# Router rows, embedding weights and bias rows in other buffers, a fifth raw buffer, and the router's products of four token tiles interleaved

## Chip, cores and metric

The kernel runs on one core of a Trainium2 chip. The metric is device microseconds of one execution; the time of a kernel is the median of its runs. TensorE (PE) does the matrix products, VectorE (DVE), ScalarE (ACT) and GpSimd (POOL) the work on their results; SyncE (SP) issues most of the loads. The launch covers two layers of a transformer trunk, 512 tokens of width 1024, everything in fp32.

## The reference, cut to what matters

```python
for i in range(DEPTH):                       # 2 layers
    a = rmsnorm(h, g_mix[i])
    proj = a @ w_in[i]                       # q, k, v of three head groups
    oa = axial_gqa(qa, ka, va)               # group a
    ob = neighbourhood_attn(qb, kb, vb, na_bias[i])   # group b: relative bias
    oc = dilated_mixture(qc, kc, vc)         # group c
    h = h + concat(rmsnorm(oa), rmsnorm(ob), rmsnorm(oc)) @ w_out[i]
    h = h + expert_choice_ffn(rmsnorm(h, g_ffn[i]), w_router[i], w_gate[i], w_up[i], w_down[i])
    gate = sigmoid(rmsnorm(h, g_ple[i]) @ w_ple_gate[i])
    h = h + gate * (p[i] @ w_ple_proj[i])    # per-layer embedding, 256 -> 1024

def expert_choice_ffn(h, w_router, w_gate, w_up, w_down):
    aff = softmax(h @ w_router)              # 512 tokens x 16 experts
    gates, idx = top_k(aff.T, 64)            # each expert chooses 64 tokens
    xg = h[idx]
    hid = silu(xg @ w_gate) * (xg @ w_up)
    return segment_sum((hid @ w_down) * gates, idx)
```

The queries and keys of every head are normalized by their root mean square first. Group b adds a bias that depends on the distance of query and key and is cut by a mask.

## The kernel before

A layer is one long program, written in the order in which TensorE is to do it.

The input projection goes in seven blocks (cq, ck, cv, a, bq, bk, bv). A block (`Project`, L379) runs over 8 parts of the depth and 4 token tiles, with three matmuls for each, into banks 0 to 3. The three are there because a weight part is split into a rounded high part (a cast on ScalarE, L350) and the rest (a subtraction on POOL, L351); the pieces are the tiles `ch`, four of them. When a token tile of a q or k block is complete, `fin_qk` (L548) takes it out of its bank: a square into a "square" tile (2 buffers, L552), from which VectorE forms sums, and a copy into a "raw" tile (4 buffers, L550 and L553), which the transposes of the heads read later. The next block needs the same bank. The softmax work of the groups c, a and b is woven in behind the matmuls as side items.

Group b's bias is made on POOL (`prep_b`, L856): for each pair of heads an add of bias rows and a mask piece. The bias rows of the six heads are one tile of 1590 columns ("heads"), loaded by POOL at the layer's start (L874); the three mask pieces lie in two "square" buffers and one "w" buffer and are loaded by SP (L879). The calls stand in `bias_b`, at step 5 of block bv (`BIAS_AT`).

The output projection follows in six pieces (po[0] to po[5]). Behind its last piece stands the router: `router_T` (L934) transposes a half of one token tile of h and copies it into one of two half slots `hs`; `router_mm` (L951) multiplies the eight parts of one token tile by the router's weights, 32 columns of weights at a time. The four token tiles take the four column groups of the array, `tile_position=(0, 32 * t)`, and write to four strips of bank 0. `tail` (L960) calls both as token tiles become ready, and L984 to L986 do the rest. The logits are copied out of the bank (L1010), become probabilities, and VectorE and TensorE rank the tokens of each expert (L1037, L1050).

The experts come in eight pairs, each with 12 weight chunks of 2 MB (gate, up, down, four each). TensorE uses a chunk for 8 fp32 matmuls of 512 columns, 16 instructions in the trace. The class `Slots` plans the loads: one list of wanted chunks (`plan`, L267), a buffer ("slot") for each, and a load on SP's queue (L144) as soon as a slot is free for the first of the list. There are 9 slots of their own and two that are lent once the attention's memory is free ("early", "lent"). `keep(n)` holds back n half slots from the list, `take` hands out a half slot, `give` returns it. The load of the embedding's weights (1 MB, key "pp") stands in the same list ahead of pair 5, since `ple_proj` (L1139) uses them in that pair, on half slots too: one for the input and its transposes, two for the result.

## Time and profile before

| | |
|---|---|
| median of 3 runs | 1619.06 us (1618.86 to 1619.22) |
| the profiled execution's own time | 1618.79 us |
| its span in the profile | 1617.0 us (the other 1.8 us lie around it) |
| mean granted clock of TensorE | 0.986 |
| busy: TensorE, its weight loads | 1528.5 us (95%), 877.6 us (54%) |
| busy: VectorE, ScalarE, POOL | 713.1 us (44%), 489.1 us (30%), 278.9 us (17%) |
| moved by DMA | 469.81 MB, mean 291 GB/s |
| chain that ended last | TensorE 22%, DMA 12%, VectorE 3% |

The page's table of slices divides the span into 40 pieces of 40.4 us, which show the stages of both layers. Below that the trace has rows of single instructions, grouped where the same line follows itself: the time at which a group starts, how long it lasts, and in brackets the idle time of the engine ahead of it with what ended that. A fp32 matmul with 128 columns shows as two instructions ("passes"), so the router's 32 matmuls of a layer are 64 in the trace. A share over the whole span is a mean over these stages, so each stage is read by itself.

### The profile page before, as it was taken

Reading aid. Unit: us, or ns where it says so; the run is one execution under the profiler, and the core shown is the slowest. Engines: PE = TensorE matmul, PEld = TensorE weight load, DVE = VectorE, ACT = ScalarE, POOL = GpSimd, SP = SyncE. Lnnn points to the kernel's source line nnn. Section 1 sums busy time; section 2 is a strip of 40 time slices with the busy share of each in tenths; the row PEclk is TensorE's granted clock in tenths of the full one; section 3 lists DMA queues with packets and bytes.
Section 4 is the critical chain, followed back from the end, with each engine's and each line's share of the span. In section 5 each row is a group of like instructions: output and inputs, shape, how many; then the busy total and the mean of one; then the engine's idle time right before and its main releaser. Section 6 shows DMA issues by size and latency. Waiting matters only on the chain. (4 is left out here: it accounts for less than half of the span.)

```text
span 1617.0 us, 20229 instructions
## 1 busy us (share of the span) xinstructions
PE 1528.5 (95%) x7819; PEld 877.6 (54%) x7819; DVE 713.1 (44%) x1885; ACT 489.1 (30%) x1151; POOL 278.9 (17%) x282
## 2 busy tenths in 40 slices
PE   7999999999999987998999999998999998889988
PEld 7866777633443333333898677775344342333346
DVE  4757856442442322221476678563432342222143
ACT  6466545201101002011664655442101000021044
POOL 4413344000000000000544133530000000000013
PEclk9999999899999999999999999999999999899999
DMA  8003154899999999999401122468999999999961
GB/s 308 20 21 114 34 197 171 327 395 428 426 427 427 428 426 428 427 428 422 159 33 40 40 94 65 166 260 338 418 427 427 428 427 428 425 427 427 427 261 52
DMA packets 46176, 469.81 MB, mean 291 GB/s; under 512 B 7104, under 2 KB 9088, under 8 KB 19456
## 3 DMA queue, kind: packets, MB, share of 16 engines
q1 hardware_dynamic: 41296, 454.15, 68.6%
q0 software_dynamic: 3744, 13.16, 2.2%
q10 hardware_dynamic: 1040, 1.21, 0.3%
q8 instruction: 61, 1.00, 0.2%
q14 instruction: 35, 0.29, 0.1%
HBM read 461.04 MB, written 6.29 MB: 289 GB/s over the span
## 5 line engine op out<-in xcount | busy, mean ns | idle before, releaser
L235 PE MATMUL bank<-slots,xt 128*64 128x512 f32 x2048 | 460.6, 602 | 21.4 <-DMA slots<-in_w_up_dram 13.6
L235 PE MATMUL bank<-ch,slots 128*128 128x384 f32 (+1 forms) x2064 | 472.2, 372 | 8.0 <-ACT raw L553 5.3
L235 PEld LDWEIGHTS bank<-ch,slots 128*128 128x128 f32 x2064 | 360.2, 189 | 83.4 <-issue 38.9
L235 PEld LDWEIGHTS bank<-slots,xt 128*64 128x64 f32 x2048 | 143.9, 138 | 308.5 <-issue 272.3
L351 POOL TENSOR_TENSOR ch<-slots,ch 128x384 fp32r<-128x384 f32 (+1 forms) x172 | 199.8, 1169 | 328.9 <-ACT ch L350 304.8
L235 PE MATMUL bank<-slots,hid 128*64 128x512 f32 x1024 | 227.4, 598 | 13.1 <-DMA slots<-in_w_down_dram 10.0
L235 PEld LDWEIGHTS bank<-slots,hid 128*64 128x64 f32 x1024 | 72.6, 137 | 156.8 <-issue 139.6
L1195 DVE SCALAR_TENSOR_TENSOR hid<-bank,st,hid 128x512 f32<-128x512 f32 x32 | 23.8, 750 | 283.5 <-PE bank L235 274.6
L1086 POOL DMA_INDIRECT xg<-rows,ids x14 | 13.8, 986 | 724.1 <-DVE ids L1059 638.7
L350 ACT CAST ch<-slots 128x384 fp32r<-128x384 f32 (+1 forms) x172 | 95.5, 563 | 87.5 <-PE bank L235 64.7
L1130 DVE TENSOR_TENSOR h<-h,bank 128x512 f32<-128x512 f32 x128 | 79.9, 682 | 84.8 <-PE bank L235 84.8
L1229 DVE SCALAR_TENSOR_TENSOR xg<-bank,st,hid 128x512 fp32r<-128x512 f32 x32 | 22.6, 746 | 212.3 <-ACT hid L1228 212.3
L1191 ACT ACTIVATE hid<-bank,st 128x512 f32<-128x512 f32 x32 | 22.0, 687 | 264.5 <-PE bank L235 264.5
L235 PE MATMUL bank<-slots 64*128 64x512 f32 (+2 forms) x304 | 93.9, 558 | 0.9 <-DVE sa L679 0.9
L1037 DVE SCALAR_TENSOR_TENSOR less<-bank,tgv,order 128x512 bf16<-128x512 f32 x128 | 87.6, 747 | 15.8 <-PE bank L238 15.8
L1098 ACT ACTIVATE xt<-bank,gcols 128x128 f32<-128x128 f32 x56 | 20.4, 367 | 204.5 <-PE bank L238 202.8
L681 ACT ACTIVATE p<-p,sa 128x512 f32<-128x512 f32 (+1 forms) x96 | 58.8, 613 | 72.8 <-DVE sa L679 72.6
L1228 ACT ACTIVATE hid<-bank,st 128x512 fp32r<-128x512 f32 x32 | 20.3, 684 | 177.2 <-issue 144.1
L356 DVE SCALAR_TENSOR_TENSOR slots<-bank,gcols,slots 128x128 fp32r<-128x128 f32 (+1 forms) x160 | 53.4, 373 | 44.6 <-ACT slots L355 44.1
L238 PE MATMUL bank<-ident,p 128*128 128x128 f32 x416 | 63.0, 274 | 3.6 <-ACT slots L608 3.0
L355 ACT ACTIVATE slots<-bank,gcols 128x128 fp32r<-128x128 f32 (+1 forms) x160 | 53.9, 400 | 29.7 <-PE bank L235 18.2
L238 PEld LDWEIGHTS bank<-ident,p 128*128 128x128 f32 x416 | 50.5, 140 | 15.7 <-ACT slots L608 3.7
(139 smaller groups left out, 1442.8 us busy)
## 6 DMA issues: line engine op xcount, KB each, us to landing
slots<-in_w_gate_dram SPq DMA_DIRECT2D x64, 2048.0 KB, 28.4
slots<-in_w_up_dram SPq DMA_DIRECT2D x64, 2048.0 KB, 31.2
slots<-in_w_down_dram SPq DMA_DIRECT2D x64, 2048.0 KB, 32.4
slots<-in_w_in_dram SPq DMA_DIRECT2D x24, 768.0 KB, 5.8
slots<-in_w_ple_gate_dram SPq DMA_DIRECT2D x8, 1024.0 KB, 33.1
slots<-in_w_out_dram SPq DMA_DIRECT2D x6, 1024.0 KB, 6.0
slots<-in_w_in_dram SPq DMA_DIRECT2D x4, 1024.0 KB, 11.5
rows<-h POOLq DMA_DIRECT2D x8, 512.0 KB, 4.6
```

The source lines that it names most:

```text
L235: return placed(T.matmul(*a, **k))
L238: return placed(T.transpose(*a))
L350: S.copy(hi.bitcast(F32R), src)
L351: G.tensor_tensor(lo.bitcast(F32R), src, hi, ALU.subtract)
L355: S.activation(hi.bitcast(F32R), b, AF.Copy, scale=g)
L356: V.scalar_tensor_tensor(lo.bitcast(F32R), b, g, hi, ALU.mult, ALU.subtract)
L681: S.activation(pv, pv, AF.Exp, bias=nm, scale=-1.0, accum_out=ls)
L1037: V.scalar_tensor_tensor(ph.pool.tile([128, 512], BF16, tag="less", name="less", bufs=2), bk[6 + j], aff[:, t, e:e + 1], order[:, 128 * (3 ...
L1130: V.tensor_tensor(h[:, t, 512 * c:512 * c + 512], h[:, t, 512 * c:512 * c + 512], b, ALU.add)
L1191: S.activation(hid[:, c], bk[c], AF.Silu, scale=rslot[:, pr:pr + 1])
L1195: V.scalar_tensor_tensor(hid[:, c], bk[2 + c], rslot[:, pr:pr + 1], hid[:, c], ALU.mult, ALU.mult)
L1229: V.scalar_tensor_tensor(y[1][:, c], bk[4 + c], gatec[:, pr:pr + 1], y[0][:, c].bitcast(F32), ALU.mult, ALU.subtract)
```

## The change

Four things move, in both layers.

1. The embedding's weights leave the list of chunks. They get a tile of their own ("pp", 2048 columns) in the experts' phase, loaded on SP's queue at the start of that phase (L1007 of the new kernel).
2. `fin_qk` has five raw buffers. The bias rows no longer have a tile: they use two "square" and four "raw" buffers, and two of the mask pieces the values tile "va" of group a. So their loads stand in block bv, behind the last readers of these buffers, and the second pair's bias work moves from step 5 to step 7 of bv. The shifted values `vsh` get three tiles of their own.
3. The router's transposed rows get a phase and two tiles of their own ("rows0", "rows1"), in place of two half slots; no half slots are held back for them.
4. `router_mm` does all four token tiles in one go, the part outside, the token tile inside, so that neighbouring matmuls go to different column groups. It is called once, when all transposes are done.

```diff
--- before.py
+++ after.py
@@ -289,8 +289,6 @@
                      w_out[l, 128 * s:128 * s + 128, :].rearrange("(k q) f -> q k f", q=64)) for s in range(2)])
         mat(("out",), w_out[l], (1,))
         for e in range(0, NE, 2):
-            if e == 2 * EMBED:
-                chunks(("pp",), w_ple_proj[l])
             for name, w in (("g", w_gate), ("u", w_up), ("d", w_down)):
                 for i in range(4):
                     slots.want((l, name, e, i), [(lambda t: t, w[l, e // 2, i])])
@@ -547,7 +545,7 @@
 
         def fin_qk(t):
 
-            raw[t] = pa.tile(384, "raw", 4)
+            raw[t] = pa.tile(384, "raw", 5)
             sq = pa.tile(384, "square", 2)
             S.activation(sq, bk[MAIN[t]][:, 0:384], AF.Square)
             S.copy(raw[t], bk[MAIN[t]][:, 0:384])
@@ -856,29 +854,30 @@
         def prep_b(hd):
             bm = bmt[hd % 2]
             for i, off in ((0, 248), (1, 256), (2, 264)):
-                src = bias["raw"][:, hd, :]
+                src = bias["raw"][hd]
                 sv = bass.AP(tensor=src.tensor, offset=src.offset + off, ap=[list(src.ap[0]), [-1, 32], [-31, 8]])
                 G.tensor_tensor(bm[:, 256 * i:256 * i + 256].rearrange("q (j r) -> q j r", r=8), sv,
                                 bias["mask"][i].rearrange("q (j r) -> q j r", r=8), ALU.add)
 
         bmt = [pa.tile(768, f"bias{i}") for i in range(2)]
-        bias["raw"] = pa.tile(1590, "heads").rearrange("q (a n) -> q a n", a=6)
+        vsh = [pa.tile(384, f"shift{i}") for i in range(3)]
 
         def bias_b():
 
             side.drain()
             slots.give(ptx.pop())
             bias["vbt"] = slots.take()
-            bias["mask"] = [pa.tile(384, n, b)[:, 0:256] for n, b in (("square", 2), ("square", 2), ("w", 1))]
+            bias["raw"] = [pa.tile(384, n, b)[:, 0:265] for n, b in [("square", 2)] * 2 + [("raw", 5)] * 4]
+            va2 = pa.tile(512, "va")
+            bias["mask"] = [va2[:, 0:256], va2[:, 256:512], pa.tile(384, "w")[:, 0:256]]
             for hd in range(6):
-                G.dma_start(out=bias["raw"][:, hd, :],
+                G.dma_start(out=bias["raw"][hd],
                             in_=bass.AP(tensor=na_bias.tensor,
                                         offset=na_bias.offset + l * (NABIAS + 2 * BPAD) + BPAD + 465 * hd - 16,
                                         ap=[[1, 16], [31, 8], [1, 265]]))
             for i in range(3):
                 nc.sync.dma_start(out=bias["mask"][i], in_=cst_maskb[:, 256 * i:256 * i + 256])
             prep_b(0)
-            prep_b(1)
 
         def fin_vb(t):
             if "v" not in bias:
@@ -888,9 +887,8 @@
 
         layer.fin["bv"] = fin_vb
         now, late = post_qk(0, 6, 2, "b", 0, bqk[1])
-        pj["bv"].run(merge(then, now, {BIAS_AT: [bias_b]}))
+        pj["bv"].run(merge(then, now, {BIAS_AT: [bias_b], 7: [lambda: prep_b(1)]}))
         vb = bias["v"]
-        vsh = [pa.tile(384, "raw", 4) for i in range(3)]
         for i in range(3):
             S.dma_start(out=vsh[i][0:64, :], in_=vb[64:128, i, :])
             S.dma_start(out=vsh[i][64:128, :], in_=vb[0:64, i + 1, :])
@@ -934,8 +932,6 @@
         sh = ph.tile(8, "sh").rearrange("q (f t) -> q f t", f=2)
 
         def router_T(t, f):
-            if not hs:
-                hs.extend(slots.take() for _ in range(2))
             b = bk[1 + (t + f) % 3]
             for j in range(4):
                 k = 4 * f + j
@@ -948,10 +944,13 @@
             S.activation(unused(512), h[:, t, 512 * f:512 * f + 512], AF.Square,
                          accum_out=sh[:, f, t:t + 1])
 
-        def router_mm(t):
+        def router_mm():
+
             for k in range(8):
-                mm(bk[0][32 * t:32 * t + 32, 0:128], wr[:, k, :], four(hs[k // 4])[:, k % 4, 128 * t:128 * t + 128],
-                   start=k == 0, stop=k == 7, tile_position=(0, 32 * t))
+                for t in range(4):
+                    mm(bk[0][32 * t:32 * t + 32, 0:128], wr[:, k, :],
+                       four(hs[k // 4])[:, k % 4, 128 * t:128 * t + 128],
+                       start=k == 0, stop=k == 7, tile_position=(0, 32 * t))
 
         def free_b(n):
             if n > 11:
@@ -961,8 +960,6 @@
             G.dma_start(out=rows[128 * t:128 * t + 128, :], in_=h[:, t, :])
             if t > 0:
                 router_T(t - 1, 1)
-            if t > 1:
-                router_mm(t - 2)
 
         group["b"] = Attention("b", six(*bqk), [ptx[0][:, 512 * i:512 * i + 512] for i in range(4)])
         side.start(group["b"].items(free_b, group["a"].scale), PACE[2], LEAD[2])
@@ -978,20 +975,23 @@
         pa.close()
         phY = Phase("early", "right")
         slots.lend(phY.pool, NEARLY)
-        slots.keep(2)
+        slots.keep(0)
+        phR = Phase("router")
+        hs.extend(phR.tile(2048, f"rows{f}") for f in range(2))
         po[4].run({2: [group["b"].scale]}, po[5])
         po[5].run({i: [lambda t=t: router_T(t, 0) for t in ((0, 1), (2,), (3,))[i]] for i in range(3)})
         router_T(3, 1)
-        router_mm(2)
-        router_mm(3)
+        router_mm()
         slots.give(*mts[2:])
         if stop == "attn":
+            phR.close()
             break
 
 
         V.tensor_scalar(sh[:, 0], sh[:, 0], 1.0 / D, EPS, ALU.mult, ALU.add)
         V.scalar_tensor_tensor(ms4, sh[:, 1], 1.0 / D, sh[:, 0], ALU.mult, ALU.add)
         rsqrt(rtok, ms4, ta4, tb4)
+        phR.close()
         ph.close()
         phT = Phase("pt")
         pos = phT.tile(64, "pos").rearrange("q (t e) -> q t e", t=4)
@@ -1000,10 +1000,11 @@
         phX = Phase("lent")
         slots.lend(phX.pool, NLENT)
         ph = Phase("moe")
-        slots.give(*hs)
         slots.keep(0)
         G.iota(tgv[:, :, 0], pattern=[[128, 4]], base=0, channel_multiplier=1,
                allow_small_or_imprecise_dtypes=True)
+        wpp = ph.tile(2048, "pp")
+        nc.sync.dma_start(out=wpp, in_=w_ple_proj[l, 0])
         iot = ph.tile(64, "iot")
         G.iota(iot, pattern=[[1, 64]], base=0, channel_multiplier=0, allow_small_or_imprecise_dtypes=True)
         lg = ph.tile(512, "oh")[:, 0:128]
@@ -1137,7 +1138,7 @@
                 S.copy(pT[:, k, :], bk[6 + k])
 
         def ple_proj():
-            wp = slots.get((l, "pp", 0)).rearrange("q (k f) -> q k f", k=2)
+            wp = wpp.rearrange("q (k f) -> q k f", k=2)
             n = 0
             for t in range(4):
                 for f in range(2):
@@ -1147,7 +1148,6 @@
                         mm(b, pT[:, k, 128 * t:128 * t + 128], wp[:, k, 512 * f:512 * f + 512],
                            start=k == 0, stop=k == 1)
                     S.copy(ppv(t, f), b)
-            slots.done((l, "pp", 0))
 
         def halves(t):
             return t.rearrange("q (c n) -> q c n", c=2)
```

TensorE's order at the router of layer 0, before (bank_64 is bank 0 with the logits, bank_71 the output projection's last bank, `h` the transposes' source, slots_2569 the router's rows):

```order
L238 MATMUL bank_67<-ident,h 128x128 x4
L235 MATMUL bank_64<-slots_2569,wr 32x128 x8
L235 MATMUL bank_71<-ch,slots_908 128x512 x3
L238 MATMUL bank_65<-ident,h 128x128 x4
L235 MATMUL bank_64<-slots_2569,wr 32x128 x12
L238 MATMUL bank_66<-ident,h 128x128 x4
L235 MATMUL bank_64<-slots_2569,wr 32x128 x12
L238 MATMUL bank_69<-ident,oh 128x128
```

and now:

```order
L238 MATMUL bank_67<-ident,h 128x128 x4
L235 MATMUL bank_71<-ch,slots_908 128x512 x3
L235 MATMUL bank_64<-rows_2512,wr 32x128
L238 MATMUL bank_65<-ident,h 128x128 x4
L235 MATMUL bank_64<-rows_2512,wr 32x128 x4
L238 MATMUL bank_66<-ident,h 128x128 x4
L235 MATMUL bank_64<-rows_2512,wr 32x128 x11
L235 MATMUL bank_64<-rows_2513,wr 32x128 x16
L238 MATMUL bank_69<-ident,oh 128x128
```

The eight matmuls of the first two token tiles that stood ahead of bank_71's last three products are gone from there; 27 of the 32 now stand behind the last transposes (bank_66), where 12 stood.

ScalarE's order at the end of block bk (L552 and L553 are the square and the copy of `fin_qk`, bank_67 its last token tile, L672 exponentials of another group), before:

```order
L745 ACTIVATE squares<-bank_70 128x256
L350 CAST ch<-slots_110 128x384
L552 ACTIVATE square<-bank_67 128x384
L350 CAST ch<-slots_110 128x384
L319 ACTIVATE sa<-sa 128x24
L320 ACTIVATE sa<-sa 128x24
L672 ACTIVATE p,sa<-bank_68,sa 128x512
L672 ACTIVATE p,sa<-bank_69,sa 128x512
L553 COPY raw<-bank_67 128x384
L708 COPY slots_754<-bank_70 128x4x128
```

and now, where the same lines are two lower:

```order
L743 ACTIVATE squares<-bank_70 128x256
L348 CAST ch<-slots_110 128x384
L550 ACTIVATE square<-bank_67 128x384
L551 COPY raw<-bank_67 128x384
L348 CAST ch<-slots_110 128x384
L317 ACTIVATE sa<-sa 128x24
L318 ACTIVATE sa<-sa 128x24
L670 ACTIVATE p,sa<-bank_68,sa 128x512
L348 CAST ch<-slots_571 128x384
L670 ACTIVATE p,sa<-bank_69,sa 128x512
L706 COPY slots_754<-bank_70 128x4x128
```

The copy into raw has moved up to its square; before, it stood behind a cast, two small activations and two exponentials. The same move is found at the ends of ck and bq. POOL's order in block bv is, before (L351 are splits of weight parts, L861 the bias adds):

```order
L351 TENSOR_TENSOR ch<-slots_110,ch 128x384 x2
L351 TENSOR_TENSOR ch<-slots_571,ch 128x384 x4
L351 TENSOR_TENSOR ch<-slots_110,ch 128x384 x4
L861 TENSOR_TENSOR bias_1714<-heads,square 128x256
L861 TENSOR_TENSOR bias_1715<-heads,square 128x256
L351 TENSOR_TENSOR ch<-slots_571,ch 128x384 x2
```

and now:

```order
L349 TENSOR_TENSOR ch<-slots_571,ch 128x384 x4
L349 TENSOR_TENSOR ch<-slots_110,ch 128x384 x2
L874 DMA square<-in_na_bias_dram 128x1x265
L349 TENSOR_TENSOR ch<-slots_110,ch 128x384 x2
L874 DMA square<-in_na_bias_dram 128x1x265
L859 TENSOR_TENSOR bias_1714<-square,w 128x256
L859 TENSOR_TENSOR bias_1715<-square,w 128x256
L349 TENSOR_TENSOR ch<-slots_571,ch 128x384
L874 DMA raw<-in_na_bias_dram 128x1x265
L349 TENSOR_TENSOR ch<-slots_571,ch 128x384 x3
L874 DMA raw<-in_na_bias_dram 128x1x265
```

The bias rows' loads and the first pair's adds (with the mask piece "w", before at about 151 us) now stand between the splits of bv.

SP's order from the hand-over to the experts, before (the slots' numbers only tell buffers apart):

```order
L144 DMA slots_2503<-in_w_up_dram 128x4096
L144 DMA slots_2567<-in_w_up_dram 128x4096
L144 DMA slots_2702<-in_w_down_dram 128x4096
L144 DMA slots_2720<-in_w_down_dram 128x4096
L144 DMA slots_2725<-in_w_down_dram 128x4096
L144 DMA slots_2797<-in_w_down_dram 128x4096
L144 DMA slots_2821<-in_w_gate_dram 128x4096
L144 DMA slots_2841<-in_w_gate_dram 128x4096
```

and now:

```order
L144 DMA slots_2507<-in_w_up_dram 128x4096
L144 DMA slots_2572<-in_w_up_dram 128x4096
L144 DMA slots_2578<-in_w_down_dram 128x4096
L144 DMA slots_2712<-in_w_down_dram 128x4096
L144 DMA slots_2731<-in_w_down_dram 128x4096
L1007 DMA pp<-in_w_ple_proj_dram 128x2048
L144 DMA slots_2808<-in_w_down_dram 128x4096
L144 DMA slots_2832<-in_w_gate_dram 128x4096
```

The embedding's weights stand behind three "down" chunks of the first pair; before, they stood between a "down" chunk and the first "gate" chunk of pair 5.

## Rows read from the trace of the kernel before

**Rows 1.** Page, mean DMA rate in the span's 40 slices of 40.4 us

```profile
GB/s 308 20 21 114 34 197 171 327 395 428 426 427 427 428 426 428 427 428 422 159 33 40 40 94 65 166 260 338 418 427 427 428 427 428 425 427 427 427 261 52
```

**Rows 2.** Windows: length, busy of PE, PEld, DVE, ACT, POOL; clock, DMA share, GB/s

```profile
292.00:293.00 1.00, 1.00 (x7) 0.77 (x6) 1.00 (x2) 0.24 (x1) 0.03 (x1) 1.00 0.00 0
305.00:310.00 5.00, 3.10 (x13) 2.70 (x14) 3.70 (x11) 0.70 (x1) 0.00 (x0) 0.50 1.02 433
317.00:318.00 1.00, 1.00 (x8) 0.41 (x6) 0.00 (x0) 0.00 (x0) 0.00 (x0) 1.00 0.00 0
320.00:325.00 5.00, 5.00 (x29) 2.36 (x29) 0.00 (x0) 0.63 (x2) 0.00 (x0) 1.00 0.89 338
400.00:440.00 40.00, 40.00 (x198) 16.70 (x196) 17.33 (x49) 3.68 (x8) 0.98 (x1) 1.00 1.01 427
720.00:760.00 40.00, 36.15 (x167) 11.99 (x168) 3.87 (x12) 2.86 (x5) 0.00 (x0) 1.00 1.01 426
1105.00:1110.00 5.00, 3.04 (x16) 2.80 (x15) 5.00 (x17) 0.00 (x0) 0.00 (x0) 0.69 1.02 435
```

**Rows 3.** Timeline of SP's queue: start, us, load, count

```profile
296.95 22.32 SPq L144 DMA_DIRECT2D slots<-in_w_down_dram  x4
...
503.31 10.20 SPq L144 DMA_DIRECT2D slots<-in_w_up_dram  x3
...
537.67 0.33 SPq L144 DMA_DIRECT2D slots<-in_w_ple_proj_dram  x1
```

**Rows 4.** Timeline of TensorE near the end of layer 0's experts

```profile
757.15 3.65 PE L235 MATMUL bank<-slots,hid 128*64 128x512 f32 x16 [1.17 <-DMA slots<-in_w_down_dram]
```

**Rows 5.** Page, DMA issues: count, size of one, median us to landing

```profile
slots<-in_w_up_dram SPq DMA_DIRECT2D x64, 2048.0 KB, 31.2
```

**Rows 6.** TensorE's waits (total, times, longest), and timelines at block bk's end

```profile
PE bank L235 <- ACT raw L553: 5.3, 6, 1.4
...
192.01 0.47 ACT L553 COPY raw<-bank 128x384 f32<-128x384 f32 x1
...
192.53 0.80 PE L235 MATMUL bank<-ch,slots 128*128 128x384 f32 x3 [1.38 <-ACT raw L553]
```

**Rows 7.** Timelines of TensorE and VectorE at layer 0's router

```profile
294.09 1.93 PE L235 MATMUL bank<-slots,wr 128*32 128x128 f32 x16
295.95 0.97 PE L235 MATMUL bank<-ch,slots 128*128 128x512 f32 x3
...
299.62 0.66 PE L238 MATMUL bank<-ident,h 128*128 128x128 f32 x4
300.21 2.40 PE L235 MATMUL bank<-slots,wr 128*32 128x128 f32 x24
...
296.96 0.75 DVE L911 SCALAR_TENSOR_TENSOR h<-bank,sa,h 128x512 f32<-128x512 f32 x1 [2.09 <-PE bank L235]
```

**Rows 8.** Groups by line and shape: count, busy, mean ns, idle before

```profile
L235 PE MATMUL bank<-tgv,pick 128*128 128x18 f32 x128 | 15.8, 257 | 3.5 <-DVE pick L1050 3.5
L235 PE MATMUL bank<-slots,wr 128*32 128x128 f32 x128 | 13.5, 274 | 0.0
L235 PE MATMUL bank<-slots,raw 128*64 128x128 f32 x96 | 8.4, 280 | 0.0
L235 PEld LDWEIGHTS bank<-slots,wr 128*32 128x32 f32 x128 | 11.9, 110 | 1.0 <-issue 1.0
```

**Rows 9.** Timelines of POOL and TensorE in bv; landing of the bias rows (L874)

```profile
194.00 1.01 POOL L351 TENSOR_TENSOR ch<-slots,ch 128x384 fp32r<-128x384 f32 x1 [3.62 <-ACT ch L350]
...
208.03 1.33 PE L235 MATMUL bank<-ch,slots 128*128 128x384 f32 x6
...
DMA to landing us min/median/max: 4.6/6.1/7.7
```

**Rows 10.** Timelines of TensorE at the rank behind the router, layers 0 and 1

```profile
308.87 6.33 PE L235 MATMUL bank<-pick,h 128*128 128x128 f32 x28 [1.73 <-DVE pick L1050]
...
1107.21 4.88 PE L235 MATMUL bank<-pick,h 128*128 128x128 f32 x28 [1.96 <-DVE pick L1050]
```

## Prediction, made before the change was run

> **What bounds the kernel now.** I read the slices of the page first, to see which of the two long resources is short where. Each of the two layers has a stretch of about 400 us at 422 to 428 GB/s, and before it four slices of attention, 160 us, with 20 to 114 GB/s [rows 1]. Then I cut windows at the borders of these stretches [rows 2]: between 400 and 440 us the DMA engines are busy the whole time (share 1.01, 427 GB/s), and at 720 to 760 they still are (426 GB/s), while TensorE has 3.85 us of gaps in 40. Ahead of that, 292 to 293 and 317 to 318 show DMA share 0 while TensorE is full, and 320 to 325 only 338 GB/s. So each layer has three regimes: attention, where TensorE's order counts and DMA hardly; the hand-over to the experts (about 290 to 340 us in layer 0), where loads wait for buffers; and the expert stream, where only bytes count. The loads on SP's queue say why [rows 3]: from 296.95 to 319 us four loads go out, as slots come free; in the stream three issues 10.20 us apart from first to last (the last itself takes 0.33) are 4.93 us per 2 MB chunk, which is 2.10 MB at 427 GB/s, and TensorE ends the stretch waiting for chunks that have just landed [rows 4].
>
> This gives the prices: a byte in the stream costs its time at 427 GB/s, a byte in the hand-over is free while the engines have gaps, and a microsecond that TensorE saves between attention and the first expert moves the start of the stream and counts in full.
>
> **The change, part by part.** The sum is made against the profiled execution, 1618.79 us, which is 0.27 below the median of 1619.06. What a measurement of this kernel can tell from no change is about 0.2%, 3.2 us.
>
> *Embedding weights.* One load of 1 MB per layer leaves the stream, where it stood at 537.67 us [rows 3], and goes out ahead of the experts, behind the loads of the hand-over on SP. Out of the stream it saves 1.05 MB at 427 GB/s, 2.46 us. In its new place it takes 2.46 us of engines that stood idle around 317 and ran at 338 GB/s after 320: 20 us at 338 instead of 427 GB/s leave room for 1.8 MB. Nothing is due there: SP's next load waits for TensorE to release a slot anyway. Two layers: **-4.9**. Bounds: 0 (the stream waits for something else) and -4.9.
>
> *One weight slot more ahead of the router, one fewer behind pair 5.* The router's transposed rows no longer sit in half slots, so one "down" chunk can go out some 18 us sooner and fill the gap at 292 us. But the chunks that fit before TensorE frees the first one are as many as before (before, the router's slot came back as soon as its products were read), so the stream's start isn't moved: 0. Behind pair 5 the embedding's three half slots now keep a second slot open. A chunk is issued a median of 31.2 us ahead of its landing [rows 5], six spacings of 4.93; five in the queue feed the engines as well: 0.
>
> *Fifth raw buffer.* In the profile's waits TensorE stops six times for ScalarE's copy into a raw buffer, 5.3 us in all [rows 6]: the order shows the copy pushed behind a cast, two small ops and two exponentials for want of a buffer, so it ends at 192.48 and TensorE, which needs the bank, starts 1.38 us late at 192.53. With five buffers the copy stands next to its square. All six are at the end of a q or k block. I take the whole, **-5.3**; the exponentials behind it move back by one copy of 0.47, and the attention items that use them run beside the projection, so I add nothing. Bounds: 0 and -5.3.
>
> *Router.* Before, 64 passes per layer (32 fp32 matmuls of two passes) run in pieces of 16, 24 and 24 between the transposes, and the last piece, 24 in 2.40 us, ends at 302.61 [rows 7]. Now, by the order, 10 passes stand between the transposes and 54 behind the last of them. The 16 passes ahead of the last three projection matmuls go, so these end 1.9 us sooner, at about 295.1. VectorE's residual of 0.75 is then through at 295.9. TensorE meanwhile has 10 passes and the transposes of the third token tile (0.66), and then those of the fourth: with 0.7 for the passes, they end at about 297.1. What a pass costs when neighbours go to four column groups, no row shows. In one column group it is 105 ns (13.5 us for 128) [rows 8]. Two alternating halves of 64 columns take 88 ns per pass, a full-width stream 123: 35 ns less for 64 columns fewer. Another 32 fewer would be 17.5 less, so I take 70 ns. Then 54 passes are 3.8 us, the end is 300.9, 1.7 sooner, **-3.4** in two layers. Bounds: 105 ns, if the interleaving buys nothing, ends at about 303.1 (the first ten passes too at the full price), +0.5 per layer, +1.0; 26 ns, four at once, ends at about 298.1, -4.5 per layer, -9.0. By the Trainium skill, TensorEngine Tiling (Array Packing), Overview, four tiles of 32 columns run side by side at up to four times the speed; by that the sum would be 5.6 us lower than mine. The trace has two halves at 1.4 times the full width, not 2.
>
> *Bias rows, masks.* The six bias-row loads per layer leave the layer's start and stand on POOL inside block bv, between its splits; the first bias piece now waits for a square buffer. Such a load lands in 6.1 us (4.6 to 7.7) [rows 9]. That puts the two bias adds ahead of the split that ran at 194.00, which would end at about 197.3 instead of 195.0; TensorE uses it at 208.03. Ten microseconds of cover: 0. Without that cover each microsecond of lateness on POOL would be one on TensorE. The second and third bias pieces and the masks move back by some 8 us, ahead of first use at about 230: 0.
>
> *The rank behind the router* finds TensorE's clock lowered, and not alike in both layers: a mean of 0.50 of full speed from 305 to 310 us, which is 1.2 GHz, and 0.69 from 1105 to 1110, a mix of 1.2 and 2.4 [rows 2]; its 28 matmuls took 6.33 and 4.88 us [rows 10]. Ahead of it TensorE waits for VectorE in both. An earlier start may change either layer: 1.5 per layer in both directions, for the range.
>
> Sum: -4.9 - 5.3 - 3.4 = -13.6. 1618.79 less 13.6 is 1605.2; with the 0.27 between profile and median, **1605.5 us**.
>
> **Rivals.**
> *Interleaving buys nothing.* A pass stays at 105 ns, and the block of 54 lies behind the last transpose, with nothing beside it. For it: 128 columns at 105 ns is the price of one column group at work, and full-width passes with weight loads aren't cheaper. Against: the 88 ns of two halves. -4.9 - 5.3 + 1.0 = -9.2: 1609.9.
>
> *Four at once*, 26 ns. For it: with 512 columns the halves do run nearly so. Against: at 128 columns they don't, and a weight load of 110 ns goes with each pass [rows 8]. -4.9 - 5.3 - 9.0 = -19.2: 1599.9.
>
> *Raw gaps move on.* TensorE gets its bank sooner and stops at the next split instead. For it: in bv, POOL waits 3.62 us for ScalarE's cast [rows 9]. Against: TensorE's waits name the copy alone. -4.9 - 3.4 = -8.3: 1610.8.
>
> *The load was hidden anyway.* If the stream is held by slots and not by bytes at 537 us, the first term is gone: 1610.4. Against: share 1.01.
>
> *Weight loads that aren't covered.* Then a pass in the interleaved block is matmul plus load, 105 + 110 = 215 ns [rows 8], 54 take 11.6 us, the end is 308.7, +6.1 per layer: -4.9 - 5.3 + 12.2 = +2.0, 1621.1, inside the 0.2%. Against: in one column group too each pass has its load, and takes 105 in all. The Trainium skill has a rule that would make it so: TensorE: Matmul & The Clock Gate, on what overlaps in tile positions, says that a weight load overlaps running matmuls only where the row group differs, and here all four tiles have the same rows. The trace disagrees for one column group: 13.5 us for 128 passes and their 128 loads of 110 ns.
>
> *Slower: POOL stuck on its bias row.* The first add stands in POOL's order ahead of the splits that TensorE needs. If the row lands not in 6.1 us but as a weight chunk does behind a full queue, in 31.2 [rows 5], the split ends 25.1 us later than reckoned, 14 of them beyond the cover (208.03 less 197.3 is 10.7): +28.8 in two layers, 1634. It decides against the gains from a landing of about 24 us on (6.1 + 10.7 + 6.8). Against: the slice from 160 to 200 us, in which the loads now fall, moves 34 GB/s [rows 1].
>
> **How the numbers follow.** Forecast 0.45; interleaving buys nothing 0.14; four at once 0.12; raw gaps move on 0.10; load hidden 0.05; two of these shortfalls together 0.05 (1614.8 to 1615.7, at the edge of the 0.2%, so half of it counts as no change); uncovered loads 0.02 (within); POOL stuck 0.04, slower; something slower that I haven't named 0.03. Faster 0.45 + 0.14 + 0.12 + 0.10 + 0.05 + 0.025 = 0.885, say 0.88; same 0.045, say 0.05; slower 0.07. The range runs from four at once with a little of the clock's help, 1599, to the two one-sided shortfalls at 1610 to 1611 with the rank's clock the wrong way, 1613. That leaves out 0.14 by cases and a few hundredths at the edges.
>
> **What would show it.** Right: TensorE's waits have no line for the copy into raw; the 1 MB load goes out near 303 to 319 us and the chunks around 537 us follow each other at 4.9 us; the passes of the router's block are near 70 ns and end about 301; the split in bv ends near 197 and nobody waits for it. Wrong: a wait of TensorE for a split where the copy was; a stream that ends no sooner though it has 1 MB less; passes at 105 ns or over; POOL waiting for a bias row beyond 10 us; or a first expert that starts sooner while the stream ends as before, which would say that the hand-over was held by slots.

## The result: 1598.55 us, 20.6 less than before

The changed kernel takes 1598.55 us in the median (1598.17 to 1600.14, 4 runs), against 1619.14 for the kernel before on the same chip (1618.86 to 1619.69): a ratio of 0.9874, 95% interval 0.9857 to 0.9891. It is faster, as forecast, by 20.6 us and not by 13.6, and it lies 0.45 us under the range. The profiled execution took 1598.17 us, its span is 1596.4.

### Where the time went

Both timelines of TensorE, cut at the same instructions (the second set of transposes of the input; the end of the last projection matmul ahead of the router; the end of the last router pass; the first expert's first matmul; the end of the last expert's last chunk). In layer 1 the attention's stretch begins at layer 0's last chunk and so holds the end of layer 0 too:

| stretch, us | before, layer 0 / 1 | after, layer 0 / 1 | difference, both |
|---|---|---|---|
| start, to the input's second transposes | 10.73 | 7.96 | -2.8 |
| attention | 286.19 / 335.12 | 282.52 / 331.09 | -7.7 |
| router, behind the last projection matmul | 5.69 / 5.69 | 3.60 / 3.60 | -4.2 |
| logits and rank | 12.64 / 10.72 | 11.98 / 11.80 | +0.4 |
| expert stream | 445.56 / 445.42 | 442.71 / 441.88 | -6.4 |
| end | 59.26 | 59.26 | 0 |

They add up to the 20.6 us between the spans.

The router after, TensorE's timeline of layer 0 (start, length, instruction, count):

```profile
289.53 0.95 PE L235 MATMUL bank<-ch,slots 128*128 128x512 f32 x3
290.40 0.41 PE L235 MATMUL bank<-rows,wr 128*32 128x128 f32 x2
290.74 0.66 PE L238 MATMUL bank<-ident,h 128*128 128x128 f32 x4
291.33 0.43 PE L235 MATMUL bank<-rows,wr 128*32 128x128 f32 x8
291.69 0.66 PE L238 MATMUL bank<-ident,h 128*128 128x128 f32 x4
292.27 1.81 PE L235 MATMUL bank<-rows,wr 128*32 128x128 f32 x54
...
306.06 3.65 PE L235 MATMUL bank<-slots,xt 128*64 128x512 f32 x16
```

It is the order that was read ahead of the run, 2, 8 and 54 passes, and 54 of them take 1.81 us, a mean of 34 ns, where the mean of a pass was 105 [rows 8]. The projection's last three matmuls (289.53) come directly on the ones ahead of them; the 16 passes of [rows 7] that took 1.93 us are gone from there.

The waits of TensorE after (total, times, longest):

```profile
PE bank L235 <- DMA slots<-in_w_up_dram: 14.6, 13, 2.0
PE bank L235 <- DMA slots<-in_w_down_dram: 11.6, 10, 2.5
...
PE bank L235 <- DMA slots<-in_w_gate_dram: 3.1, 2, 1.9
...
PE bank L238 <- ACT slots L706: 2.7, 2, 1.5
```

The line for the copy into raw, 5.3 us in [rows 6], is gone. Two waits for another copy of ScalarE are new (L706, a copy of transposed probabilities). TensorE's timeline at the end of block bk shows one of them where the 1.38 us stood before:

```profile
186.05 1.31 PE L235 MATMUL bank<-ch,slots 128*128 128x384 f32 x6
188.85 0.66 PE L238 MATMUL bank<-ident,p 128*128 128x128 f32 x4 [1.49 <-ACT slots L706]
```

SP's queue after, and windows of the hand-over and the stream at the places of [rows 2]:

```profile
277.74 16.74 SPq L144 DMA_DIRECT2D slots<-in_w_down_dram  x3
294.58 0.38 SPq L1007 DMA_DIRECT2D pp<-in_w_ple_proj_dram  x1
309.75 0.33 SPq L144 DMA_DIRECT2D slots<-in_w_down_dram  x1
```

```profile
284.00:285.00 1.00, 1.00 (x6) 0.81 (x5) 0.00 (x0) 0.19 (x1) 0.00 (x0) 1.00 1.07 459
309.00:310.00 1.00, 1.00 (x7) 0.36 (x4) 0.00 (x0) 0.00 (x0) 0.00 (x0) 1.00 0.65 270
312.00:317.00 5.00, 5.00 (x30) 2.41 (x29) 0.00 (x0) 0.63 (x2) 0.00 (x0) 1.00 1.02 387
391.00:431.00 40.00, 40.00 (x198) 16.62 (x196) 17.31 (x49) 3.80 (x9) 0.97 (x1) 1.00 1.00 427
```

The embedding's weights go out at 294.58. The gaps of the DMA engines are nearly closed: share 1.07 where [rows 2] had 0 at 292 us, 0.65 where it had 0 at 317, and 1.02 in place of 0.89 behind that. The stream runs at 427 GB/s as before.

The start was not in the forecast. TensorE's timeline before, and then after:

```profile
10.73 1.97 PE L238 MATMUL bank<-ident,h 128*128 128x128 f32 x8 [3.62 <-DMA h<-in_x_dram]
```

```profile
7.96 1.97 PE L238 MATMUL bank<-ident,h 128*128 128x128 f32 x8 [0.76 <-DMA h<-in_x_dram]
```

The second half of the input arrives 2.8 us sooner, since POOL no longer loads six bias rows at that moment.

### The profile page after: what moved, and what is told of

It reads as the page before. It is cut to its first block, busy times and chain, and to the rows that moved or that the text cites. A ratio compares the mean times of both kernels' runs of the same rounds, so it can differ in the third digit from the quotient of the medians.

```text
span 1596.4 us, 20220 instructions
## 1 busy us (share of the span) xinstructions
PE 1514.5 (95%) x7819; PEld 867.3 (54%) x7819; DVE 710.4 (45%) x1885; ACT 488.6 (31%) x1151; POOL 276.5 (17%) x282
## 4 chain that ended last, share of the span: by engine, by line
PE 65%; DMA 22%; DVE 8%; ACT 4%; issue 1%; POOL 0%; SPq 0%; ACTq 0%; DVEq 0%
PE bank L235 59%; DMA slots<-in_w_down_dram 9%; DMA slots<-in_w_up_dram 7%; PE bank L238 5%; DMA slots<-in_w_gate_dram 5%; DVE less L1038 1%; ACT p L679 1%; DVE raw L537 1%; DVE p L677 1%; DVE p L687 1%; DVE h L909 1%; DVE slots L708 0%; ACT p L685 0%; ACT slots L353 0%; ACT ch L348 0%
## 5 line engine op out<-in xcount | busy, mean ns | idle before, releaser
L235 PE MATMUL bank<-slots 64*128 64x512 f32 (+2 forms) x240 | 63.1, 535 | 0.9 <-DVE sa L677 0.9
```

Of the source, the lines that this page charges most:

```text
L235: return placed(T.matmul(*a, **k))
```

## The experiments

All are compared by medians of 4 to 11 runs. Medians of one kernel differ by about 1 us from one set of runs to another (1598.55 and 1597.54 for the changed kernel), so small differences are read from the traces, cut as in the table above. Each kernel has the trace of one execution.

### What a router pass costs

```diff
 # router_one_group
-            for k in range(8):
-                for t in range(4):
+            for t in range(4):
+                for k in range(8):
 # router_two_groups
-            for k in range(8):
-                for t in range(4):
+            for k, t in [(k, t) for u in (0, 2) for k in range(8) for t in (u, u + 1)]:
```

> The changed kernel with the router's 32 products in one go, but all eight parts of one token tile first, then the next: neighbours stay in one column group. Theory A (neighbours in four column groups run side by side, and that alone makes a pass cost 34 ns): the 54 passes take 54 x 105 ns = 5.7 us instead of 1.81, the first expert starts 3.9 us later in each layer, about 7.7 us in all, 1606.3 us. Rival B (one unbroken block of passes is cheap wherever they go, since nothing stands between them): the passes stay at 34 ns, 1598.5 us.

> The same, but with two token tiles interleaved and then the other two. Theory A: a pass costs half of 105 ns, 53 ns, 54 of them 2.8 us, 1.0 us more per layer, 1600.6 us. Rival C (my forecast's rule, by which the price falls by a fixed step with the width and not with the number of groups): about 70 ns or more, 3.8 us, 2.0 us more per layer, 1602.5 us. Rival B: 1598.5 us.

Measured: 1605.76 us with one group, 1602.27 with two. TensorE's longest piece of the router in layer 0, first with one group, then with two (start, length, count):

```profile
292.98 5.52 PE L235 MATMUL bank<-rows,wr 128*32 128x128 f32 x60
```

```profile
293.47 3.06 PE L235 MATMUL bank<-rows,wr 128*32 128x128 f32 x58
```

The one-group block is as unbroken as the other, and its passes take 5.52/60 = 92 ns (it ends 3.7 us later behind the last projection matmul than with four groups); with two groups they take 3.06/58 = 53 ns, with four 34. These means still hold the end of a piece's last pass, 0.27 us, and the changes from one token tile to the next. The starts of the single passes in the traces are plainer. Within one token tile a pass starts 109 ns after the one before it. With two groups, two passes start 7 ns apart, and the next two 109 ns after them. With four, four start within 20 to 25 ns, and the next four 109 ns after the first, 27 ns each. So two or four passes in different column groups go for the price of one, and rivals B and C fall.

The median with two groups, 1602.27, is nearer to rival C's 1602.5 than to theory A's 1600.6; the trace decides between them. In it the router is 1.24 us longer per layer than with four groups, where theory A had 1.0 and rival C 2.0.

### The router alone

```diff
 # before_router: the kernel before, with
-        router_mm(2)
-        router_mm(3)
+        router_mm()          # parts outside, token tiles inside; none in tail
```

> The kernel before with the router's products interleaved in one go, and nothing else changed. Theory (the router is worth what the traces show between the last projection matmuls and the last router pass, 4.1 us in layer 0 and 4.8 in layer 1, and the saturated stream starts sooner by as much): -8.5 to -9, about 1610.3 us. Rival (the stream of the kernel before is held by its bytes from before the router on, so that the earlier first expert only waits for chunks): -4 or less, 1615 us.

Measured: 1610.83 us, beside 1619.56 before: -8.7. In its trace the attention is 1.6 and 2.1 us shorter (the 16 passes that left) and the router 2.1 in each layer, 7.9 in all. By the median a sooner first expert is not lost in the stream. The trace by itself doesn't show this: it is of an execution of 1614.61 us, while the other four took 1609.39 to 1611.02; its mean granted clock is 0.981 where it was 0.986 before, and its expert stream is 1.2 and 2.0 us longer.

### The embedding's weights

```diff
 # pp_in_list; pp_at_pair_2 with e == 4 (left out: ple_proj takes the slot and returns it)
+            if e == 2 * EMBED:
+                chunks(("pp",), w_ple_proj[l])
-        wpp = ph.tile(2048, "pp")
-        nc.sync.dma_start(out=wpp, in_=w_ple_proj[l, 0])
 # rows_in_slots (left out: two half slots are held back for them, and come back ahead of the experts)
+                hs.extend(slots.take() for _ in range(2))
-        hs.extend(phR.tile(2048, f"rows{f}") for f in range(2))
```

> The changed kernel with the embedding's weights back in the list of chunks ahead of pair 5, everything else as changed. Theory (bytes in the saturated stream cost their time at 427 GB/s, and nothing else): 2.46 us per layer, +4.9, 1603.5 us. Rival A (the two traces show 3.1 and 3.5 us won behind pair 4, so the half slot that the load holds counts too): +6.6, 1605.1 us. Rival B (hidden): 1598.5 us.

> The changed kernel with the embedding's weights in the list of chunks, but ahead of pair 2 and not of pair 5. At pair 2 TensorE still has chunks in stock, so no stop of 3 to 4 us follows the load. Theory (the load's price is its bytes, 2.46 us per layer, and the rest of the 6.1 us that it cost ahead of pair 5 is the long stop before that pair's first gate chunk, after which TensorE's clock is low for that chunk, 6.51 us for 16 passes in place of 3.65): about +4.9 on the changed kernel. Rival (the stop has no price of its own, the stream is late by bytes and slots alone): +6 or more here too, since the half slot is held longer.

> The changed kernel with the router's transposed rows in two half slots again, which come back at the start of the experts' phase; the interleaved products stay. Theory (the chunk that goes out 18 us sooner only fills idle engines, since TensorE's first release is the next limit): within 1 us of 1598.5. Rival (the earlier chunk moves the saturated stream's start, and is part of the 3.1 and 3.5 us won behind pair 4): up to 1.3 us more per layer, 1601 us.

> The changed kernel itself once more, beside the other three, so that they are compared on one chip. All theories: 1598.5 us, with what the rank's clock adds, up to 1601.

Measured: 1604.64 us with the load ahead of pair 5, 1604.74 ahead of pair 2, 1600.31 with the rows in slots, 1597.54 for the changed kernel again. So the place in the list makes no difference, and by the medians the load costs 6 to 7 us in either, against 4.9 by its bytes. TensorE's timeline at pair 5's first gate chunk, with the load ahead of pair 5 and then ahead of pair 2:

```profile
572.21 6.51 PE L235 MATMUL bank<-slots,xt 128*64 128x512 f32 x16 [3.73 <-DMA slots<-in_w_gate_dram]
```

```profile
571.47 3.65 PE L235 MATMUL bank<-slots,xt 128*64 128x512 f32 x16 [1.25 <-DMA slots<-in_w_gate_dram]
```

The long stop and the slow matmuls behind it are gone at pair 2, and by the medians the time isn't: my theory of that stop falls. From the last router pass to the last chunk the stretch is 454.7 and 453.7 us in the changed kernel, 457.1 and 457.1 with the load ahead of pair 2, 459.0 and 457.0 ahead of pair 5: 2.4 to 4.3 per layer.

How much of this is the load can be read from the landings of a layer's 96 chunks, each counted from the last router pass and set against the same chunk in the changed kernel. At the load they jump by 2.2 and 2.5 us when it stands ahead of pair 2, and by 2.5 and 2.4 ahead of pair 5. Between the kernel before and the changed kernel they jump by 2.5 and 2.3, at pair 5 too. So at either place the load costs its bytes, 2.46 us. The rest comes at other chunks, in steps of up to 1.5 us that go both ways; between the two traces of the changed kernel such steps reach 0.8. What makes them, and why the medians give 6 to 7, the runs don't settle. By the trace it isn't the slot that the router's rows took, since taking that again (rows_in_slots) leaves the two stretches at 453.8 and 454.7. But the four runs of that kernel lie at 1599.0 (two) and 1601.6 (two), and the trace is of one at 1599.0; by the median it lies 1.8 to 2.8 us above the changed kernel, beyond the theory's 1 us.

### The start

```diff
 # start_loads_3, start_loads_6: the changed kernel, layer 0 only (left out: early, six pieces of free tiles)
+            for hd in range(3):          # or 6
+                G.dma_start(out=early[hd], in_=<bias rows of head hd>)
 # start_wide_load
+            G.dma_start(out=bmt[0], in_=w_ple_proj[0, 0][:, 0:768])
```

> The changed kernel with six further loads of bias rows on POOL at the start of layer 0, into buffers that are free then (nothing reads them). Theory (the six loads at the start stood in the way of the loads of the input and of the first weights, by their bytes on the DMA engines: 0.8 MB at about 400 GB/s are 2 us, and their small pieces more): the second half of the input's transposes starts near 10.7 us again instead of 8.0, and the whole kernel is 2.8 us longer, 1601.3 us. Rival (the start differs for another reason, or the lateness is made up before the first block ends): 1598.5 us.

> The changed kernel with three further loads of bias rows at the start of layer 0 in place of six. Theory (what counts is the bytes ahead of the input's tiles; all three go out by 3.7 us, as the first three did before, ahead of the input's last landing): nearly the whole of what six cost, 1600 to 1601.3 us. Rival (the cost is the later issues that stand between POOL's splits from 11 us on): 1598.5 us.

> The changed kernel with one further load on POOL at the start of layer 0, 128 rows of 768 columns (0.39 MB in pieces of 3 KB; nothing reads them), in place of three bias rows (0.40 MB in pieces of 1 KB). Theory (bytes on the DMA engines delay the input): 1.0 us at about 400 GB/s, second half of the input's transposes near 9 us, +1. Rival (the many small pieces are what costs): less, +0.5 or nothing. Second rival (any load from POOL's queue at this moment costs the same, whatever it moves): the 11.3 us of three bias rows again, +3.

Measured: 1600.80 us with six rows, 1602.38 with three, 1601.36 with the wide load. All are slower than the changed kernel, but by 2 to 5 us with 1 us between sets of runs, so the medians don't put the three in order, and the traces must. TensorE's second transposes with six rows, with three, and with the wide load:

```profile
11.25 1.97 PE L238 MATMUL bank<-ident,h 128*128 128x128 f32 x8 [3.93 <-DMA h<-in_x_dram]
```

```profile
11.29 1.97 PE L238 MATMUL bank<-ident,h 128*128 128x128 f32 x8 [3.81 <-DMA h<-in_x_dram]
```

```profile
9.56 1.97 PE L238 MATMUL bank<-ident,h 128*128 128x128 f32 x8 [2.10 <-DMA h<-in_x_dram]
```

Three rows cost what six do, so the later three don't matter. The wide load moves as much as three rows and holds the transposes up by 1.6 us in place of 3.3. The queue of POOL's loads in the first 12 us, with three rows and with the wide load (packets, MB, share of the 16 engines' time):

```profile
q0 software_dynamic: 144, 0.41, 19.5%
```

```profile
q0 software_dynamic: 80, 0.39, 12.9%
```

These shares are 2.3 and 1.5 us of all engines. So for the same bytes the rows take half as much again of the engines' time, while they hold the input up twice as long. The rows differ from the wide load in their length of 1 KB, in coming as three loads and not one, and in overlapping each other in memory; no run tells these apart. The windows from 2 to 12 us say the same, with three rows, with the wide load, and in the changed kernel (last columns: DMA share, GB/s):

```profile
2.00:12.00 10.00, 2.94 (x13) 2.46 (x14) 1.54 (x6) 3.51 (x9) 4.66 (x9) 1.00 0.97 309
```

```profile
2.00:12.00 10.00, 4.20 (x17) 3.31 (x17) 2.18 (x9) 4.56 (x13) 4.50 (x7) 1.00 0.98 361
```

```profile
2.00:12.00 10.00, 4.48 (x18) 3.60 (x19) 3.26 (x13) 5.62 (x18) 3.90 (x4) 1.00 1.00 396
```

The DMA engines are equally busy and move 309 GB/s with the three bias rows among the loads, 396 without.

### Raw buffers and bias moves

```diff
 # raw_four: the changed kernel, with
-            raw[t] = pa.tile(384, "raw", 5)
+            raw[t] = pa.tile(384, "raw", 4)      # and four where the bias rows use them
 # before_bias_moves: the kernel before with item 2 of the change, but four raw buffers
 # before_bias_raw_five: the same with five
```

> The changed kernel with four raw buffers. Theory (the copies' waits were real, but part of the 5.3 us was given back to later waits): TensorE's waits name the copy into raw again, and the time rises by what the two traces show at the ends of the q and k blocks, 1.5 us in layer 0 and 2.2 in layer 1, to about 1602.2 us. Rival: all of 5.3, 1603.9 us. Second rival: the gaps have only moved, 1598.5 us.

> The kernel before with the bias rows, masks and shifted values moved as in the change, but four raw buffers; router and embedding weights as before. Theory (the start gives 2.8 us, and in the attention the bias rows, which then live in the raw buffers, make the copies wait longer: the changed kernel with four buffers lost 3.2 us per layer, where both steps together gained 1.9): the stretch from the input to the last projection is 1.0 to 1.3 us longer per layer, and -2.8 + 2.5 = about 0, 1618.5 us. Rival (the moves cost nothing in the attention): -2.8, 1616 us.

> The same with five raw buffers. Theory (together they give 1.9 us per layer and the start 2.8): -6.6, 1612.2 us. Rival (the fifth buffer gives all the waits back, 5.3, as I forecast): -8.1, 1610.7 us.

Measured: 1604.92 us with four buffers in the changed kernel; 1620.81 for the bias moves alone (ratio 1.0007, interval 0.9998 to 1.0016); 1613.16 for them with five buffers, both beside 1618.47 before. The bias moves gain 2.9 at the start and lose it again: the attention is 3.6 and 1.5 us longer. TensorE's waits in that kernel, its timeline at the end of bk, and a window there (columns as in [rows 2]; the third from the right is the granted clock):

```profile
PE bank L235 <- ACT raw L553: 6.1, 6, 1.9
```

```profile
190.82 0.80 PE L235 MATMUL bank<-ch,slots 128*128 128x384 f32 x3 [1.90 <-ACT raw L553]
...
192.32 2.08 PE L235 MATMUL bank<-slots 64*128 64x512 f32 x4
```

```profile
191.00:195.00 4.00, 4.00 (x13) 2.14 (x14) 2.34 (x5) 0.77 (x2) 1.81 (x2) 0.57 0.86 193
```

The wait for the copy is 1.90 us where it was 1.38, and behind it TensorE's granted clock is a mean of 0.57, near 1.2 GHz: four matmuls take 2.08 us that took 1.13 before. This trace is of the longest of eleven executions, 1621.91 us. A stop as long isn't always followed by that; in the changed kernel with four buffers TensorE's timeline at the same place and the window from 191 us are

```profile
190.62 0.79 PE L235 MATMUL bank<-ch,slots 128*128 128x384 f32 x3 [1.94 <-ACT raw L551]
...
191.78 1.13 PE L235 MATMUL bank<-slots 64*128 64x512 f32 x4
```

```profile
191.00:195.00 4.00, 4.00 (x24) 2.81 (x22) 3.36 (x8) 1.91 (x6) 1.89 (x3) 1.00 0.82 181
```

With five buffers the wait and the fall of the clock are both gone. The fifth buffer is worth more behind the bias moves (7.6 us by the medians; 6.4 in the changed kernel, where the theory had 3.7 and the rival 5.3) than the waits of the kernel before show, and the runs don't settle why. The two steps together give 5.3 us by the medians, less than the theory's 6.6 and the rival's 8.1: in the trace 2.7 at the start, and 0.8 and 2.0 in the two layers' attention.

### A version that might have been faster

```diff
 # copies_swapped
-                if n % 2 == 0:
+                if n % 2 == (self.kind == "a"):
                     S.copy(dst, four(b))
```

> The changed kernel with the copies of group a's transposed probabilities dealt the other way round between ScalarE and VectorE, so that the copy for which TensorE now stops at the end of block bk (1.49 and 1.25 us) goes to VectorE. Theory (the gap of the raw copy has moved to this copy at bk, because both stand behind the same exponentials on ScalarE): that wait goes, and the time falls by up to 2.7 us, to 1596. Rival (TensorE then stops for the exponentials' own results, or for a copy elsewhere): no change.

Measured: 1599.04 us, no gain. The waits say why:

```profile
PE bank L238 <- DVE slots L708: 2.7, 4, 1.2
```

2.7 us again, in four pieces, now for VectorE's copies of the same transposes: 1.18 and 0.83 us at the end of bk, and 0.35 us twice some 13 us later.

## Why the prediction was right and wrong

*Router: right in mechanism, mis-sized from a row that was misread.* The step that failed is "Two alternating halves of 64 columns take 88 ns per pass", with "so I take 70 ns", which follows from it by a fixed amount per column. The 88 ns are busy time over count [rows 8], of passes that come in pieces of about eight, and a piece counts until its last pass has ended, 0.27 us after that pass began. One such piece in the trace of before:

```profile
244.41 0.60 PE L235 MATMUL bank<-slots,raw 128*64 128x128 f32 x8
```

In it two passes start 6 ns apart and the next two 109 ns after them, 55 ns each, half of the 109 from pass to pass in one column group. So two halves did run at twice the speed at 128 columns too. The 123 ns beside it, "a full-width stream", is of a stream of 18 columns, in pieces of eight as well. Read from start to start, this row shows two halves at half the price, and the same rule carried on to four groups gives 27 ns, which the rival "four at once" had (26). It is what the passes now take from start to start; with the piece's end the mean is 34. The last pass ends 3.6 us behind the last projection matmul, where the forecast had 5.8 (300.9 less 295.1), and the router is worth -7.9 in two layers where I had -3.4 and the rival -9.0. The Trainium skill (TensorEngine Tiling (Array Packing), Overview) has up to four times the speed for four tiles; the trace agrees, with 109 ns for one pass and for four. The Trainium skill's rule on weight loads (TensorE: Matmul & The Clock Gate, What overlaps and what doesn't), that one overlaps running matmuls only where the row group differs, doesn't hold here: 54 passes with their 54 loads take 1.81 us though all four tiles have the same rows.

*The start: a step that wasn't there.* I wrote that the six loads "leave the layer's start" and costed only where they go. They had competed with the input's tiles, for which TensorE waited 3.62 us before and 0.76 after. This is worth 2.8 us, where the forecast had 0, and it alone takes the result out of the range, whose lower end was the rival "four at once" with a little of the clock's help: without it the time would be near 1601.4.

*Fifth buffer: the term was too large, and a rival held in part.* "I take the whole, -5.3": of the six waits four are gone for good, and the two at the end of bk have moved to a copy behind the same exponentials, 2.7 us. "Raw gaps move on" had such a move, for all six and to a split. The attention beyond the router's share gained 2.0 + 2.0 = 4.0 (7.7 less 3.7); with the bias moves and five buffers alone it gained 2.8. So the term was 2.8 to 4.0 where I had 5.3.

*Embedding's weights: right, in cause and in size.* At the load's old place the landings jump by 2.5 and 2.3 us, 4.8 in all, where I had -4.9. The load fills idle DMA time in the hand-over, as forecast. The stream's -6.4 and the rank's +0.4 together are 1.2 more than these 4.8; that part isn't at the load, and its cause is open, as is that of the 6 to 7 us which the medians give for the load.

*Costed at nothing.* One slot more ahead of the router: right by the trace, in which the stretches are alike; by the median, 1600.31 with the rows in slots again, the 1.8 to 2.8 us above the changed kernel stay open. POOL's delay in bv: right as far as TensorE goes. POOL did wait for a bias row, 3.31 us, and the split behind it ran at 190.71. TensorE is 4.3 us ahead there, so this is 195.0 by the times of before, 1.0 later than the 194.00 of [rows 9], and TensorE uses it 13 us later without a stop:

```profile
189.90 0.85 POOL L859 TENSOR_TENSOR bias<-square,w 128x256 f32<-128x256 f32 x1 [3.31 <-DMA square<-in_na_bias_dram]
190.71 1.04 POOL L349 TENSOR_TENSOR ch<-slots,ch 128x384 fp32r<-128x384 f32 x1
...
203.77 1.33 PE L235 MATMUL bank<-ch,slots 128*128 128x384 f32 x6
```

So the slower rival had its wait, and lacked the size: the rows landed in a median of 4.6 us (3.2 to 7.2), and it needed 24. The rank's clock came out near neutral: -0.7 and +1.1.

The router's term was too small by 4.5 us and the start's by 2.8, about 1.1 came in the stream and the rank away from the load, and the fifth buffer's term was too large by 1.3: that makes up the 7 us.

## What to carry to other kernels

Products whose stationary side is 32 columns wide should be ordered so that neighbours go to different column groups; ordering alone put four passes into the 109 ns of one here. A price per instruction that is busy time over count holds the end of every piece's last instruction; where the pieces are short, read the distance from start to start instead. A load that is moved away has a price at the place that it leaves as well as at the one it goes to: look there for who waits. A wait removed on one engine is worth the distance to the next thing behind the same work on that engine, so take each single wait and ask what follows on the releasing engine.

## What was not expected of the hardware

At the start 0.40 MB in rows of 1 KB held the input up by 3.3 us and 0.39 MB in rows of 3 KB by 1.6, with the DMA engines busy for 0.97 and 0.98 of the time in both. A stop of 1.90 us in one run was followed by a stretch at a mean clock of 0.57 that cost another 1 us, while after stops of 1.38, 1.49 and 1.94 us at the same place in other kernels the clock stayed at 1.00. So the length of the stop alone doesn't tell, and the runs don't show what does.
